# Two feature tiles per VectorE and ScalarE operation in the up stage of a hybrid block, with PSUM tiles of two banks there

## The chip, the cores and the metric

The kernel runs on one core of a Trainium2 chip. The metric is device time in microseconds (us) of one execution of the whole kernel. Five engines work side by side on that core, each with its own queue of instructions, taken in order: TensorE (PE in the profile) multiplies matrices, VectorE (DVE) and ScalarE (ACT) do arithmetic on whole tiles, GpSimd (POOL) and SyncE (SP) mostly issue DMA transfers between HBM (device memory) and the core's SBUF. Engines wait for one another through semaphores. TensorE writes its products into PSUM, which this kernel divides into eight banks, each a tile of 128 partitions by 512 float32 numbers.

## The reference

One layer of a transformer block on a sequence of 256 positions with 2048 features. Cut to the part that the change and the prediction touch:

```python
x = x + merged @ w_out[l]                          # o stage; merged: three gated attention branches

h2 = rms_norm(x, g_ffn[l])
u = causal_depthwise_conv(h2 @ w_up[l], conv_w[l], conv_b[l])   # up stage: 2048 -> 2 x 5632, 3 taps
u_gate, u_val = jnp.split(u, 2, axis=-1)
x = x + (jax.nn.silu(u_gate) * u_val) @ w_down[l]  # down stage: 5632 -> 2048
```

`causal_depthwise_conv` makes each feature at position s from the same feature at positions s, s-1 and s-2 with three factors of that feature and a bias. Inputs and outputs are float32.

## The kernel before, in words

**Precision.** A float32 product is made of products of split numbers: `hi` is the number cast to the shorter type fp32r, `lo` the remainder. `piece()` (L137) brings 128x1024 weights in by one DMA of SP's queue (`raw`), lets ScalarE cast them into `hi` (L143) and VectorE subtract to get `lo` (L144). There are four buffers of each. Where weights are already on the chip or come by another way, `parts()` does the same (L378, L379).

**Stages.** The kernel works through its matrix products one after the other: the projections (names in g, f, s, b, kv), attention, the gates, the o stage (names with `o`), the up stage (names with `u`), and the down stage (names with `d`). The o and the down stage are made by `blocked()` (L423) for two column halves `nb` of 1024: some pairs of weight rows are multiplied plainly (`eight`, four accumulators X), others by a scheme with seven products in place of eight (`seven`, with four more accumulators Y). When the last product of seven is issued, `gather()` (L404) adds Y into the residual `xres`; at the end of a half L1213 adds X into `xres` on VectorE. All accumulators are PSUM banks.

**The up stage** (L1303 to L1327) goes through 11 groups of four feature tiles. For each group there are two sweeps, s=0 for the gate half of the features and s=1 for the value half. A sweep loads eight pieces of `w_up`; a piece serves two k steps (128 of the 2048 input features each) and four feature tiles. For each of these there are two matmuls: L1318 multiplies `hi` of the weights by [hi | lo] of `hT`, 512 columns (256 positions, both parts of the split), and L1319 multiplies `lo` of the weights by the hi part, 256 columns. They add up in one bank per feature tile, `u<f>_<s>`: left half and right half of a bank are two sums that have to be added. With two sweeps of four banks, all eight are in use by turns.

When a sweep is issued, one `conv` per feature tile is put into a list of side work with `later()` (L97); `tick()` (after each piece) takes the next step of it. `conv` reads the bank: ScalarE copies its right half (L1253), VectorE adds the left half (L1254), and multiplies by `rbc` (L1263), the row factor of the RMS norm, the same for all features. The result lies in `u_0` or `u_1`, tiles with two zeros ahead of position 0. Then come the taps with factors that belong to a feature: ScalarE's L1268 (third factor and bias), VectorE's L1269 and L1270. The gate half ends with SiLU (L1272). The value half is multiplied into it (L1276), and `split_to` (L175) splits the product into hi (L177) and lo (L178) for the down stage.

**What sets the order.** Most instructions stand in each queue in the order that the program issues them, fixed by `pin()` and `in_order()`. The first group is special, since `hT` and `rbc` are not ready: `hidden_T(n)` (L1176) makes a quarter of `hT`. It transposes `xres` on TensorE into banks (`transposed`, L191), and ScalarE and VectorE split it from there (L184, L186). Its last two quarters are made while the first sweep runs, as side work between pieces. After them POOL writes the row factors to DRAM and reads them back spread over all partitions: that is `rbc` (L1186, L1187).

**PSUM.** One pool `pp` of eight one-bank tiles, from the start to the end of the kernel (L81). A new tile takes the next bank in turn and waits for what was done with that one bank:

```python
    pp = ctx.enter_context(tc.tile_pool(name="pp", bufs=8, space=bass.MemoryType.PSUM))

    def bank(name):
        return pp.tile([P, 512], F32, tag="bank", name=name)
```

## Time and profile before

| | |
|---|---|
| median of three runs | 1457.79 us (1457.63 to 1458.24) |
| span of the profiled execution, the kernel's time in that execution | 1457.8 us |
| mean DMA rate | 270 GB/s |
| instructions on TensorE, VectorE, ScalarE | 7289, 1824, 1222 |
| stages by TensorE's instructions | o stage ends at 742.5, up stage 742.5 to 1232.5, down stage from there to 1453.8 |

The profiled execution's own time is its span, and that is the median to within 0.01 us. In the rows that follow, a line such as "L1318 PE MATMUL u<-hT,hi_u" names the line of the kernel, the engine, the operation, its output and its inputs (numbers of buffers left out). In a group's row the numbers behind "|" are the busy time of the group, the mean duration of one instruction in ns, the idle time of that engine just ahead of these instructions, and what ended most of that idle time. In a row of the timeline the first number is the start, the second the duration. A row of the stretches begins with the window and its length; then come busy time and count for TensorE's matmuls, its weight loads, VectorE, ScalarE and POOL, the granted clock of TensorE (1.00 is full speed), the busy share of the DMA engines, and GB/s.

### The profile page before, as it was taken

How to read it: one execution, taken by the hardware profiler on the slowest of the kernel's cores; microseconds unless marked ns; L12 is line 12 of the kernel's file. 1: busy time of each engine (PE TensorE's matmuls, PEld its weight loads, DVE VectorE, ACT ScalarE, POOL GpSimd, SP SyncE). 2: the span in 40 equal slices, each digit the busy share in tenths (PEclk: the TensorE clock that was granted, in tenths of full speed). 3: DMA queues.
4: the chain of work that ended last, by engine and by line, in shares of the span. 5: the costliest groups of instructions: out<-in, count | busy, mean ns of one | idle time of the engine just before them, and what ended most of it. 6: DMA issues, size and time to landing. Idle time of an engine off the chain costs nothing.

```text
span 1457.8 us, 20647 instructions
## 1 busy us (share of the span) xinstructions
PE 1451.5 (100%) x7289; PEld 1227.1 (84%) x7289; DVE 1229.2 (84%) x1824; ACT 857.5 (59%) x1222; POOL 33.0 (2%) x70
## 2 busy tenths in 40 slices
PE   9999999999999999999999999999999999999998
PEld 7888888888888888888888888888888888888887
DVE  5788778776898899998987988888888877999988
ACT  6755445464554555546776656556556556676775
POOL 0000011010000000000000000000000010000000
PEclk9999999999999999999999999999999999999999
DMA  8797899777668576788877888888888899789996
GB/s 296 227 350 245 324 324 328 266 247 221 206 201 272 181 219 207 264 271 254 302 226 221 294 274 300 282 276 295 284 280 291 275 260 255 253 288 341 326 334 236
DMA packets 169415, 393.41 MB, mean 270 GB/s; under 512 B 12907, under 2 KB 30207, under 8 KB 165087
## 3 DMA queue, kind: packets, MB, share of 16 engines
q1 hardware_dynamic: 165822, 384.87, 79.3%
q0 software_dynamic: 2160, 5.12, 1.8%
q10 hardware_dynamic: 1328, 2.11, 0.4%
q8 instruction: 57, 0.93, 0.2%
q14 instruction: 48, 0.39, 0.1%
HBM read 353.24 MB, written 43.00 MB: 272 GB/s over the span
## 4 chain that ended last, share of the span: by engine, by line
PE 95%; DVE 1%; issue 1%; DMA 1%; POOL 0%; ACT 0%; DVEq 0%; POOLq 0%; ACTq 0%
PE u L1318 22%; PE u L1319 11%; PE xd L386 3%; PE xd L384 3%; PE xd L385 3%; PE xg L386 3%; PE xg L384 3%; PE xg L385 3%; PE s L386 2%; PE s L384 2%; PE f L384 2%; PE f L385 2%; PE f L386 2%; PE b L386 2%; PE s L385 2%; PE b L384 2%
## 5 line engine op out<-in xcount | busy, mean ns | idle before, releaser
L1318 PE MATMUL u<-hT,hi_u 128*128 128x512 f32 x1232 | 428.4, 394 | 0.0
L1319 PE MATMUL u<-hT,lo_u 128*128 128x256 f32 x1232 | 341.3, 277 | 0.0
L144 DVE TENSOR_TENSOR lo_u<-raw_u,hi_u 128x1024 fp32r<-128x1024 f32 x176 | 215.4, 1225 | 72.4 <-ACT hi_u L143 72.3
L1318 PEld LDWEIGHTS u<-hT,hi_u 128*128 128x128 f32 x1232 | 231.0, 188 | 53.5
L143 ACT CAST hi_u<-raw_u 128x1024 fp32r<-128x1024 f32 x176 | 184.7, 1050 | 130.1 <-PE u L1318 95.5
L1319 PEld LDWEIGHTS u<-hT,lo_u 128*128 128x128 f32 x1232 | 231.3, 188 | 0.0
L379 DVE TENSOR_TENSOR lo_d<-raw_d,hi_d 128x1024 fp32r<-128x1024 f32 x88 | 106.9, 1223 | 13.2 <-ACT hi_d L378 11.1
L378 ACT CAST hi_d<-raw_d 128x1024 fp32r<-128x1024 f32 x88 | 91.8, 1054 | 36.7 <-PE xd L385 11.9
L378 ACT CAST hi_g<-raw_g 128x1024 fp32r<-128x1024 f32 (+1 forms) x80 | 77.1, 972 | 49.8 <-PE xg L385 17.0
L379 DVE TENSOR_TENSOR lo_g<-raw_g,hi_g 128x1024 fp32r<-128x1024 f32 (+1 forms) x80 | 88.8, 1122 | 4.1 <-ACT hi_g L378 4.1
L384 PE MATMUL xg<-hi_g,xT 128*128 128x512 f32 x175 | 68.1, 389 | 0.0
L386 PE MATMUL xg<-lo_g,xT 128*128 128x512 f32 x175 | 68.1, 389 | 0.0
L385 PE MATMUL xg<-hi_g,xT 128*128 128x512 f32 x175 | 68.1, 389 | 0.0
L143 ACT CAST hi_f<-raw_f 128x1024 fp32r<-128x1024 f32 (+1 forms) x40 | 38.6, 968 | 46.4 <-PE f L385 29.9
L1318 PE MATMUL u<-hT_rest,hi_u 128*128 128x512 f32 x176 | 62.0, 394 | 0.0
L1268 ACT ACTIVATE y<-u,taps 128x256 f32<-128x256 f32 x88 | 49.6, 596 | 19.0 <-DVE u L1263 18.9
L144 DVE TENSOR_TENSOR lo_s<-raw_s,hi_s 128x1024 fp32r<-128x1024 f32 (+1 forms) x40 | 44.7, 1124 | 18.5 <-ACT hi_s L143 18.5
L143 ACT CAST hi_b<-raw_b 128x1024 fp32r<-128x1024 f32 x32 | 33.7, 1053 | 45.0 <-PE b L385 21.1
L144 DVE TENSOR_TENSOR lo_f<-raw_f,hi_f 128x1024 fp32r<-128x1024 f32 (+1 forms) x40 | 44.4, 1118 | 17.1 <-ACT hi_f L143 16.9
L143 ACT CAST hi_s<-raw_s 128x1024 fp32r<-128x1024 f32 (+1 forms) x40 | 38.2, 960 | 34.3 <-PE s L385 18.8
L378 ACT CAST hi_t_d<-raw_t_d 128x1024 fp32r<-128x1024 f32 (+1 forms) x54 | 43.5, 835 | 18.7 <-PE xd L385 11.6
L378 ACT CAST hi_t_g<-t_g 128x1024 fp32r<-128x1024 f32 x30 | 31.5, 1051 | 38.9 <-PE xg L385 35.6
(555 smaller groups left out, 3552.4 us busy)
## 6 DMA issues: line engine op xcount, KB each, us to landing
raw_u<-in_w_up_dram SPq DMA_DIRECT2D x176, 512.0 KB, 5.0
raw_g<-in_w_in_dram SPq DMA_DIRECT2D x96, 512.0 KB, 4.6
raw_d<-in_w_down_dram SPq DMA_DIRECT2D x61, 512.0 KB, 5.5
pre_d<-in_w_down_dram SPq DMA_DIRECT2D x17, 1024.0 KB, 7.8
kept_d<-pre_d SPq DMA_DIRECT2D x17, 1024.0 KB, 6.5
raw_f<-in_w_in_dram SPq DMA_DIRECT2D x32, 512.0 KB, 5.7
raw_s<-in_w_in_dram SPq DMA_DIRECT2D x32, 512.0 KB, 5.8
raw_t_d<-kept_d SPq DMA_DIRECT2D x27, 512.0 KB, 5.8
```

Of the source, the lines that this page charges most:

```text
L143: pin(nc.scalar.copy(hi[:, :m], raw[:, :m]))
L144: pin(nc.vector.tensor_tensor(lo[:, :m], raw[:, :m], hi[:, :m].bitcast(F32), ALU.subtract))
L378: nc.scalar.copy(hi[:, :n], src)
L379: nc.vector.tensor_tensor(lo[:, :n], src, hi[:, :n].bitcast(F32), ALU.subtract)
L384: fix(nc.tensor.matmul(o, lhsT=ah, rhs=w[0], start=first, stop=False))
L385: fix(nc.tensor.matmul(o, lhsT=al, rhs=w[0], start=False, stop=False))
L386: fix(nc.tensor.matmul(o, lhsT=ah, rhs=w[1], start=False, stop=last))
L1268: nc.scalar.activation(y, u[:, 2:], AF.Identity, scale=tap(2), bias=tap(3))
L1318: nc.tensor.matmul(ps[i], lhsT=hi[:, j, c], rhs=hT(k + j), start=first, stop=False)
L1319: nc.tensor.matmul(ps[i][:, :S], lhsT=lo[:, j, c], rhs=hT(k + j)[:, :S], start=False, stop=last)
```

## The change

In the up stage, VectorE and ScalarE take two feature tiles in one operation wherever no factor of a single feature is in it: the copy of the right half, the addition of the left half, the multiplication by `rbc`, SiLU, the product of gate and value, and the split into hi and lo. The taps stay at one operation per feature tile. PSUM tiles in the up stage have two banks each, `[P, 2, 512]`, and the tiles `u_0`, `u_1` and `y` hold two features. The separate tile `cr` is gone: the copy writes to `u_0` or `u_1` at once.

The pool `pp` is closed ahead of the up stage and a pool `pu` with four two-bank tiles is opened (`new_banks`); `pu` is closed ahead of the down stage and `pd`, again with one-bank tiles, is opened. The four first tiles of `pu`, `first_0` to `first_3`, are taken at once. The first of the transposes of `hT` in the up stage go into `first_0` and `first_1`, and the first sweep into `first_3` and `first_2`. In the down stage Y takes the tag of one half of the pool and X that of the other, exchanged for the second column half.

```diff
@@ -78,10 +78,21 @@
     nc.gpsimd.memset(sm_pad, 0.0)
-    pp = ctx.enter_context(tc.tile_pool(name="pp", bufs=8, space=bass.MemoryType.PSUM))
-    def bank(name):
-        return pp.tile([P, 512], F32, tag="bank", name=name)
+    banks = [ctx.enter_context(ExitStack())]
+    pools = [banks[0].enter_context(tc.tile_pool(name="pp", bufs=8, space=bass.MemoryType.PSUM))]
+    def bank(name, tag="bank"):
+        return pools[0].tile([P, 512], F32, tag=tag, name=name)
+    placed = {}
+    def two_banks(i, name):
+        return placed.pop(i, None) or pools[0].tile([P, 2, 512], F32, tag=f"banks{i}", name=name)
+    def new_banks(name, n):
+        banks[0].close()
+        banks[0] = ctx.enter_context(ExitStack())
+        pools[0] = banks[0].enter_context(tc.tile_pool(name=name, bufs=n, space=bass.MemoryType.PSUM))
...
@@ -188,9 +199,9 @@
-    def transposed(dst, src, g, k, name, n=2):
-        ps = bank(f"{name}_{k}")
+    def transposed(dst, src, g, k, name, n=2, ps=None):
+        ps = bank(f"{name}_{k}") if ps is None else ps
         for j in range(n):
...
@@ -423,8 +434,10 @@
         wv = by_k(w)
-        X = [[bank(f"x{name}{nb}_{t}_{n}") for n in range(2)] for t in range(NT)]
-        Y = []
+        own = ("bank_a", "bank_b")[:: 1 - 2 * nb] if name == "d" else ("bank", "bank")
+        ys_of = lambda: [bank(f"y{name}{nb}_{j}", own[0]) for j in range(4)]
+        Y = ys_of() if name == "d" else []
+        X = [[bank(f"x{name}{nb}_{t}_{n}", own[1]) for n in range(2)] for t in range(NT)]
         ns = plan.count("s")
...
@@ -525,7 +538,7 @@
                         ready()
-                    Y += [bank(f"y{name}{nb}_{j}") for j in range(4)]
+                    Y += [] if Y else ys_of()
                 by_seven(sp[s], s == 0, s == ns - 1)
...
@@ -1175,8 +1188,12 @@
         yield 0 if n == 2 else 1
-        transposed(hT, xres, gffn, 4 * n, "hT")
-        transposed(hT, xres, gffn, 4 * n + 2, "hT")
+        at = [None, None]
+        if "up" in issued:
+            both = two_banks(n - 2, f"hT_{n}")
+            at = [both[:, i] for i in range(2)]
+        for i in range(2):
+            transposed(hT, xres, gffn, 4 * n + 2 * i, "hT", ps=at[i])
         square_part(ssf, xres, n, "f")
...
@@ -1243,63 +1260,66 @@
         for i in range(2):
-            u = cp.tile([P, S + 2], F32, bufs=1, name=f"u_{i}")
-            nc.vector.memset(u[:, 0:2], 0.0)
+            u = cp.tile([P, 2, S + 2], F32, bufs=1, name=f"u_{i}")
+            nc.vector.memset(u[:, :, 0:2], 0.0)
             pads.append(u)
...
     def out_of(ps, dst):
-        nc.scalar.copy(dst, ps[:, S:])
-        nc.vector.tensor_tensor(dst, dst, ps[:, :S], ALU.add)
+        nc.scalar.copy(dst, ps[:, :, S:])
+        nc.vector.tensor_tensor(dst, dst, ps[:, :, :S], ALU.add)
         return dst
     def y_tile(f, s):
-        return cp.tile([P, S], F32, tag="y", bufs=6, name=f"y_{f}_{s}")
+        return cp.tile([P, 2, S], F32, tag="y", bufs=3, name=f"y_{f}_{s}")
     def taken(cr, y, f, s):
-        ct = s * FT + f
-        u = pads[f % 2]
-        ins = nc.vector.tensor_tensor(u[:, 2:], cr, rbc, ALU.mult)
+        u = pads[f // 2 % 2]
+        ins = nc.vector.tensor_tensor(u[:, :, 2:], cr, rbc.unsqueeze(1).to_broadcast([P, 2, S]), ALU.mult)
         if y is not None:
         y = y_tile(f, s) if y is None else y
-        tap = lambda j: taps[:, j, ct : ct + 1]
-        nc.scalar.activation(y, u[:, 2:], AF.Identity, scale=tap(2), bias=tap(3))
-        nc.vector.scalar_tensor_tensor(y, u[:, 1 : S + 1], tap(1), y, ALU.mult, ALU.add)
-        nc.vector.scalar_tensor_tensor(y, u[:, 0:S], tap(0), y, ALU.mult, ALU.add)
+        tap = lambda j, i: taps[:, j, s * FT + f + i : s * FT + f + i + 1]
+        for i in range(2):
+            nc.scalar.activation(y[:, i], u[:, i, 2:], AF.Identity, scale=tap(2, i), bias=tap(3, i))
+        for i in range(2):
+            for j in (1, 0):
+                nc.vector.scalar_tensor_tensor(y[:, i], u[:, i, j : S + j], tap(j, i), y[:, i], ALU.mult, ALU.add)
         if s == 0:
...
             nc.vector.tensor_tensor(g, g, y, ALU.mult)
-            a_done.append(a_pair(f // 2)[:, f % 2])
+            a_done.append(a_pair(f // 2))
             split_to(a_done[-1], g)
-    def conv(ps, f, s):
-        taken(out_of(ps, cp.tile([P, S], F32, tag="cr", bufs=2, name=f"cr_{f}_{s}")), None, f, s)
-        return
-        yield
-    def first_convs(ps):
+    def convs(ps, f, s):
+        for i in range(2):
+            fi = f + 2 * i
+            taken(out_of(ps[i], pads[fi // 2 % 2][:, :, 2:]), None, fi, s)
+            yield
+    def first_convs(ps, f, s):
         kept = []
         padded()
-        for f in range(4):
-            kept.append(out_of(ps[f], y_tile(f, 0)))
-            if f % 2:
-                yield
+        for i in range(2):
+            kept.append(out_of(ps[i], y_tile(2 * i, 0)))
+            yield
         yield 3
-        for f in range(4):
-            taken(kept[f], kept[f], f, 0)
-            yield
-    def second_convs(ps):
+        for i in range(2):
+            taken(kept[i], kept[i], 2 * i, 0)
+            yield 1
+    def second_convs(ps, f, s):
         yield
-        for f in range(4):
-            deque(conv(ps[f], f, 1), 0)
-            yield 1
+        for _ in convs(ps, f, s):
+            yield 2
+    issued.add("up")
+    new_banks("pu", 1)
+    placed.update([(i, two_banks(i, f"first_{i}")) for i in range(4)])
     for f0 in range(0, FT, 4):
...
@@ -1307,7 +1327,8 @@
         for s in range(2):
-            ps = [bank(f"u{f0 + i}_{s}") for i in range(4)]
+            pairs_of = [two_banks((3, 2, 1, 0)[2 * s + i], f"u{f0 + 2 * i}_{s}") for i in range(2)]
+            ps = [pairs_of[i // 2][:, i % 2] for i in range(4)]
             c0 = s * D_FF + f0 * P
...
@@ -1320,15 +1341,12 @@
                 tick()
-            if f0 == 0:
-                later((first_convs, second_convs)[s](ps))
-                continue
-            for i in range(4):
-                later(conv(ps[i], f0 + i, s))
+            later((convs if f0 else (first_convs, second_convs)[s])(pairs_of, f0, s))
...
     dn = []
+    new_banks("pd", 4)
```

The names in the rows below: `xo1_t_n` are X of the second half of the o stage, `u0_0` to `u3_0` (before) and `first_3`, `first_2` (after) the accumulators of the first sweep of the up stage. A row ends with the engines whose semaphores the instruction waits for, a number at the end of a name is that of the buffer.

TensorE's queue where the o stage ends and the up stage begins, before:

```order
L386 MATMUL xo1_1_1_6346<-lo_o1_15_6718,mT_3_1_6043 128x512
L1318 MATMUL u0_0_6757<-hT_5957,hi_u0_0_0_6762 128x512 [waits Activation_49]
L1319 MATMUL u0_0_6757<-hT_5957,lo_u0_0_0_6763 128x256 [waits DVE_49]
L1318 MATMUL u1_0_6758<-hT_5957,hi_u0_0_0_6762 128x512
L1319 MATMUL u1_0_6758<-hT_5957,lo_u0_0_0_6763 128x256
L1318 MATMUL u2_0_6759<-hT_5957,hi_u0_0_0_6762 128x512 [waits DVE_49]
L1319 MATMUL u2_0_6759<-hT_5957,lo_u0_0_0_6763 128x256
L1318 MATMUL u3_0_6760<-hT_5957,hi_u0_0_0_6762 128x512 [waits DVE_49]
```

After, at the same place:

```order
L397 MATMUL xo1_1_1_6346<-lo_o1_15_6718,mT_3_1_6043 128x512
L1339 MATMUL first_3_6764<-hT_5957,hi_u0_0_0_6766 128x512 [waits DVE_49,PE_49,Activation_49]
L1340 MATMUL first_3_6764<-hT_5957,lo_u0_0_0_6767 128x256
L1339 MATMUL first_3_6764<-hT_5957,hi_u0_0_0_6766 128x512
L1340 MATMUL first_3_6764<-hT_5957,lo_u0_0_0_6767 128x256
L1339 MATMUL first_2_6763<-hT_5957,hi_u0_0_0_6766 128x512
```

The first product (L1318, now L1339) stands where it stood. Before, it had a wait for ScalarE's cast, and the products of the third and the fourth bank each had a wait for VectorE of their own. Now the first product has a wait for VectorE and one for TensorE's own earlier products besides, and those behind it have none.

VectorE's queue at that place, after (`xres_again` is the residual that L1230, before L1213, adds to; up to the second memset it is the order of before):

```order
L155 TENSOR_TENSOR lo_u0_0_4_6831<-raw_u0_0_4_6829,hi_u0_0_4_6830 128x1024 [waits DMAHW0_49,Activation_49]
L431 TENSOR_TENSOR e_1024_6733<-e_1024_6733,yo1_2_6465 128x512 [waits DVE_49]
L1230 TENSOR_TENSOR xres_again_5682<-xres_again_5682,xo1_1_0_6345 128x512 [waits PE_49]
L432 TENSOR_TENSOR xres_again_5682<-xres_again_5682,e_1024_6733 128x512 [waits DVE_49]
L155 TENSOR_TENSOR lo_u0_0_6_6874<-raw_u0_0_6_6872,hi_u0_0_6_6873 128x1024 [waits DMAHW1_49,PE_49,Activation_49]
L1230 TENSOR_TENSOR xres_again_5682<-xres_again_5682,xo1_1_1_6346 128x512 [waits DVE_49]
L1264 MEMSET u_0_7020 128x2x2
L1264 MEMSET u_1_7022 128x2x2
```

The last addition of the o stage, of `xo1_1_1`, stands behind five other operations here, two of them `lo_u`; it is the last use of a bank of the old pool on VectorE.

TensorE's queue where the up stage ends and the down stage begins (`xd0_t_n` are X of its first half), before:

```order
L1318 MATMUL u43_1_11540<-hT_rest_6863,hi_u40_1_14_11732 128x512
L1319 MATMUL u43_1_11540<-hT_rest_6863,lo_u40_1_14_11733 128x256
L384 MATMUL xd0_0_0_11754<-hi_d0_22_11760,aT_6753 128x512 [waits DMAHW5_49,DMAHW4_49,DMAHW6_49,DMAHW3_49,DMAHW7_49,DMAHW2_49,Activation_49]
L385 MATMUL xd0_0_0_11754<-hi_d0_22_11760,aT_6753 128x512
L386 MATMUL xd0_0_0_11754<-lo_d0_22_11761,aT_6753 128x512 [waits DVE_49]
```

After:

```order
L1339 MATMUL u42_1_11182<-hT_rest_6863,hi_u40_1_14_11360 128x512
L1340 MATMUL u42_1_11182<-hT_rest_6863,lo_u40_1_14_11361 128x256
L395 MATMUL xd0_0_0_11390<-hi_d0_22_11396,aT_6753 128x512 [waits DMAHW4_49,DMAHW5_49,DMAHW3_49,DMAHW6_49,DMAHW2_49,DMAHW7_49,DVE_49,Activation_49]
L396 MATMUL xd0_0_0_11390<-hi_d0_22_11396,aT_6753 128x512
L397 MATMUL xd0_0_0_11390<-lo_d0_22_11397,aT_6753 128x512
```

The first `xd` product had waits for ScalarE's cast and for DMAs, and has one for VectorE besides.

VectorE's queue at that place, from `lo_d0_24` on, after (`u40_1` and `u42_1` are the two tiles of the last value sweep):

```order
L390 TENSOR_TENSOR lo_d0_24_11473<-raw_d0_24_11470,hi_d0_24_11472 128x1024 [waits DMAHW4_49,PE_49,Activation_49]
L1271 TENSOR_TENSOR u_0_7020<-u_0_7020,u40_1_11181 128x2x256 [waits Activation_49]
L1279 TENSOR_TENSOR u_0_7020<-u_0_7020,rbc_5958 128x2x256 [waits DVE_49]
L390 TENSOR_TENSOR lo_d0_25_11491<-raw_d0_25_11488,hi_d0_25_11490 128x1024 [waits DMAHW5_49,PE_49,Activation_49]
L1288 SCALAR_TENSOR_TENSOR y_40_1_11415<-u_0_7020,taps_110,y_40_1_11415 128x256 [waits Activation_49] x2
L1288 SCALAR_TENSOR_TENSOR y_40_1_11415<-u_0_7020,taps_110,y_40_1_11415 128x256 [waits DVE_49] x2
L1271 TENSOR_TENSOR u_1_7022<-u_1_7022,u42_1_11182 128x2x256
L1294 TENSOR_TENSOR y_40_0_11208<-y_40_0_11208,y_40_1_11415 128x512 [waits DVE_49]
```

Here the additions that read the two last tiles of `pu` are the L1271 rows. The second of them, of `u42_1`, stands behind the first, the multiplication by `rbc`, `lo_d0_25` and four tap operations. Before, the four additions of the last four banks (L1254) stood in the same region, each behind its own copy.

## The prediction

> **What bounds the kernel now.** I read the busy totals first, then the chain of waits, the stretches, and the groups with what ended their idle time. All times are microseconds from the span's start.

> ```profile
> PE 1451.5 (100%) x7289; PEld 1227.1 (84%) x7289; DVE 1229.2 (84%) x1824; ACT 857.5 (59%) x1222; POOL 33.0 (2%) x70
> PE 95%; DVE 1%; issue 1%; DMA 1%; POOL 0%; ACT 0%; DVEq 0%; POOLq 0%; ACTq 0%
> ```

> TensorE is busy over the whole span, and 95% of the chain that ended last is TensorE's own instructions. A busy matmul row alone proves little, so the up stage needs a look of its own.

> ```profile
> 770.00:1000.00 230.00, 230.00 (x1329) 201.16 (x1328) 196.18 (x322) 138.57 (x213) 0.55 (x1) 1.00 0.84 282
> 1260.00:1450.00 190.00, 190.00 (x840) 157.29 (x839) 178.60 (x245) 131.23 (x170) 0.00 (x0) 1.00 0.90 309
> ```

> From 770 to 1000, inside the up stage, TensorE has no hole at all, at granted clock 1.00. VectorE is at 196 of 230 and ScalarE at 139 of 230. The down stage (1260 to 1450) has no hole either.

> ```profile
> L1318 PE MATMUL u<-hT,hi_u 128*128 128x512 f32 x1232 | 428.4, 394 | 0.0
> L1318 PEld LDWEIGHTS u<-hT,hi_u 128*128 128x128 f32 x1232 | 231.0, 188 | 53.5
> L143 ACT CAST hi_u<-raw_u 128x1024 fp32r<-128x1024 f32 x176 | 184.7, 1050 | 130.1 <-PE u L1318 95.5
> ```

> The up products (L1318) waited 0.0. The waiting goes the other way: ScalarE's cast of the next weight piece waited 95.5 for TensorE to free a buffer. VectorE and ScalarE run ahead by the four hi/lo buffers, so here they are not the bound.

> **The change, part by part.** *Fewer, wider operations.* Rows of today's operations, and of 128x512 ones of the same kind:

> ```profile
> L1254 DVE TENSOR_TENSOR cr<-cr,u 128x256 f32<-128x256 f32 x84 | 32.8, 419 | 0.0
> L1253 ACT COPY cr<-u 128x256 f32<-128x256 f32 x84 | 28.1, 366 | 13.8 <-PE u L1319 13.8
> L1272 ACT ACTIVATE y<-y 128x256 f32<-128x256 f32 x44 | 17.2, 415 | 6.6 <-DVE y L1270 6.3
> L255 DVE TENSOR_TENSOR pre_d<-pre_d 128x512 f32<-128x512 f32 x17 | 11.7, 690 | 0.3
> L410 ACT COPY e<-yo 128x512 f32<-128x512 f32 x2 | 1.2, 582 | 0.0
> L646 ACT ACTIVATE junk_f<-xres_again 128x512 f32<-128x512 f32 x8 | 5.0, 649 | 0.0
> ```

> VectorE has four tensor operations of this size per feature tile: two (L1254, L1263) for all 88 tiles and two (L1276, L178) for 44, 264 in all. At 0.42 each that is 110.9. After it are 132 at 0.69, 91.1: it saves about 20. ScalarE's 88 copies, 44 SiLUs and 44 casts become 44, 22 and 22; at 0.37 to 0.58 and 0.415 to 0.649 that saves about 15 (casts at the copy's price). The scaled operations (L1268 to L1270) stay 88 each. A read that crosses two PSUM banks stands in no row; it lies between one old operation (0.42) and two (0.84), and I take the 0.69 of the one-bank row. None of it is on the path, since TensorE waits 0.0 for these engines: **worth 0**. Even at 0.84, VectorE stays at its present 196 of 230, and the cover holds.

> *First new wait: the start of the up stage.* Before, each of the four banks of the first group is waited for alone. Now the first product waits for the last addition out of the old pool (L1213, `xo1_1_1`), as its order row's extra VectorE wait says; the value is the one that this addition sets. When is it done?

> ```profile
> 742.28 0.39 PE L386 MATMUL xo<-lo_o,mT 128*128 128x512 f32 x1
> 742.51 0.39 PE L1318 MATMUL u<-hT,hi_u 128*128 128x512 f32 x1
> ...
> 741.37 0.69 DVE L1213 TENSOR_TENSOR xres_again<-xres_again,xo 128x512 f32<-128x512 f32 x1
> ...
> 746.69 1.23 DVE L144 TENSOR_TENSOR lo_u<-raw_u,hi_u 128x1024 fp32r<-128x1024 f32 x1
> 747.83 0.69 DVE L1213 TENSOR_TENSOR xres_again<-xres_again,xo 128x512 f32<-128x512 f32 x1
> ```

> VectorE works without a pause from 741.37, and its order up to there is unchanged; all that it reads comes from products before 742.5. So the addition ends at 747.83 + 0.69 = 748.52, where TensorE went straight on at 742.51. It now stands for **6.0**. Queued behind it are all products; VectorE itself has 0.2 left to do. Bounds: 5.3, were the sum released at its start, and 6.7 with one operation more.

> *The transposes of hT* now come in three places instead of two, because the second half of a two-bank tile waits for VectorE's reading of the first. From the same durations, VectorE is done at about 757.3 (and 762.0 for the next), and TensorE arrives at about 757.3 (and 762.0). I take 0, and 0.5 as the upper end.

> *Second new wait: the start of the down stage.* The first `xd` product waits for L1271 (L1254 before) on the last pair, `u42_1`. Rows of before:

> ```profile
> 1231.65 0.28 PE L1319 MATMUL u<-hT_rest,lo_u 128*128 128x256 f32 x1
> 1232.34 0.28 PE L1319 MATMUL u<-hT_rest,lo_u 128*128 128x256 f32 x1
> 1232.46 0.39 PE L384 MATMUL xd<-hi_d,aT 128*128 128x512 f32 x1
> ...
> 1231.62 0.72 ACT L1253 COPY cr<-u 128x256 f32<-128x256 f32 x2 [0.40 <-PE u L1319]
> 1232.54 1.05 ACT L378 CAST hi_d<-raw_d 128x1024 fp32r<-128x1024 f32 x1 [0.20 <-PE u L1318]
> ...
> 1230.02 2.46 DVE L379 TENSOR_TENSOR lo_d<-raw_d,hi_d 128x1024 fp32r<-128x1024 f32 x2 [3.44 <-ACT hi_d L378]
> 1234.86 0.88 DVE L1269 SCALAR_TENSOR_TENSOR y<-u,taps,y 128x256 f32<-128x256 f32 x2
> ```

> In VectorE's new order L1271 of the last pair stands behind L1271 and L1279 of the pair before, one `lo_d`, and four scaled operations. The first pair's copy now waits for both its features; the product that starts at 1231.65 is the second's last, and today's copy began 0.3 after such a start, so the copy runs 1231.95 to 1232.55. The cast follows to 1233.6. VectorE: addition and multiplication 1232.55 to 1233.85 (0.6 to 0.7 each), `lo_d` (1.2) to 1235.0, four scaled operations (0.4 each, by the 0.88 for two) to 1236.65, the addition to 1237.3. TensorE would have gone on at 1232.46: it stands for **4.8**. Bounds: 4.5 if operations overlap as closely as these rows do, and 6.4 if a `raw_d` piece is late, as one was (1.6 beyond that).

> *The clock.* A hole of 5 to 6 is new for TensorE. The trace has one at its end:

> ```profile
> 1453.51 0.28 PE L386 MATMUL apart<-lo_d,a_ends 128*128 128x256 f32 x1
> 1452.00:1456.90 4.90, 1.79 (x14) 1.54 (x12) 1.80 (x3) 0.00 (x0) 0.00 (x0) 1.00 0.43 161
> 1457.10:1457.80 0.70, 0.00 (x0) 0.00 (x0) 0.00 (x0) 0.00 (x0) 0.00 (x0) 0.50 0.00 0
> 5.15 1.74 PE L781 MATMUL kv<-hi_kv,memT 128*128 128x512 f32 x4
> 6.72 0.63 PE L781 MATMUL kv<-lo_kv,memT 128*128 128x512 f32 x2
> ```

> The last product ends at 1453.8, and by 1457.1 the granted clock is 0.50: a hole of 3.3 was enough there. How long the half clock lasts after a hole no row shows directly. The nearest is the start: products began at 1.23 (L93), those from 5.15 still came 0.39 apart, and from 6.72 on 0.24. About 5.3 slow, half of it lost: 2.6. The price for one hole lies between 0 (no drop) and 3.4 (6.8 at half clock); I take **2.6 once**, for the longer hole.

> [...]

> **Sum.** 0 + 6.0 + 0 + 4.8 + 2.6 = +13.4. The profiled execution's span is 1457.8, equal to the median of the runs (1457.79), so 1457.8 + 13.4 = **1471.2**.

> **The rivals.**
> *No clock loss*: both waits, full clock. [...] Time 1457.8 + 10.8 = 1468.6.
> *A drop in both holes, or a third wait*: 1457.8 + 16.0 = 1473.8. The third wait would be VectorE's first multiplication by `rbc`, with split pieces queued behind it:

> ```profile
> 760.52 0.74 POOL L1186 DMA_DIRECT2D rstd_row<-scales  x1 [423.33 <-DVE scales L636]
> 770.68 0.55 POOL L1187 DMA_DIRECT2D rbc<-rstd_row  x1 [9.43 <-DMA rstd_row<-scales]
> rbc<-rstd_row POOLq DMA_DIRECT2D x1, 128.0 KB, 8.0
> ```

> Today rbc lands at 778.7. The later transposes push its start back by some 10, TensorE's holes by 6, so VectorE would stand about 5 there. The buffers ahead leave 0.3 to 1.5 at the next pieces: 0 is likeliest, 2 more possible.
> *Only the first wait bites* (the second is covered because ScalarE's and VectorE's queues are further ahead than I think): +6.0 to +8.6, 1463.8 to 1466.4. Against it: every operation in that sum reads or follows the last products.
> *Not slower.* If VectorE paced the products in the up stage, its 20 saved would come off: 1457.8 + 10.8 - 20 = 1448.6, and any 11 of them would make it even. The place is L144 ahead of L1319; it decides as soon as products wait for `lo_u`. Against it: 0.0 idle in L1318's row. For it only that a matmul row counts as busy what is queued; the weight loads' row shows 53.5 idle, which is the slack that one 512-wide product leaves after a 0.19 load.
> [...]
> *The change does not do what it says*: wide operations as dear as two. TensorE sees none of it, so the time stays 1471.2.

> **How the numbers follow.** Both waits and one drop 0.50 (1471.2); no drop 0.20 (1468.6); two drops or late rbc 0.16 (1473.8, up to 1476); one wait 0.07 (1465); within 0.2% of before 0.04, if the new waits are met before TensorE asks; faster 0.03. 0.2% (2.9) is about what a measurement here tells from no change. The range takes the first three with the bounds of the clock and of the second wait: 1465.0 to 1476.0. Slower 0.93, same 0.04, faster 0.03.

> **What would show it.** In the profile of the changed kernel: a hole of about 6 in TensorE ahead of the first `first_3` product, ended by VectorE's L1230; one of about 5 ahead of the first `xd`, ended by L1271; a granted clock of 0.50 for some 5 after the first; VectorE's busy time lower by about 20 and ScalarE's by 15, with TensorE's product spacing in between unchanged. I am wrong if the first product of either stage starts within 1 of the one before, if clock stays at 1.00, or if products in 800 to 1200 come closer together than before.

## The result and the profile after

| | before | changed |
|---|---|---|
| median (lowest to highest) | 1457.93 us (1457.63 to 1458.24, 4 runs) | 1474.18 us (1473.98 to 1475.40, 4 runs) |
| ratio, 95% interval | | 1.0111 (1.0099 to 1.0123) |
| span of the profiled execution | 1457.8 | 1472.2 |

The change makes the kernel 16.25 us slower. The page of the changed kernel, in its first section and its groups:

```profile
PE 1456.0 (99%) x7289; PEld 1230.6 (84%) x7289; DVE 1225.2 (83%) x1692; ACT 848.4 (58%) x1134; POOL 32.6 (2%) x70
...
L1339 PE MATMUL u<-hT,hi_u 128*128 128x512 f32 x1176 | 408.7, 394 | 0.0
...
L154 ACT CAST hi_u<-raw_u 128x1024 fp32r<-128x1024 f32 x176 | 184.8, 1051 | 148.2 <-PE u L1339 97.5
...
L395 PE MATMUL xd<-hi_d,aT 128*128 128x512 f32 x136 | 54.1, 398 | 4.8 <-issue 4.8
```

The up products still wait 0.0, and ScalarE's cast still waits for TensorE: in the middle of the stage nothing changed. New is a wait of 4.8 ahead of `xd` (L395), whose releaser the page could not name. The start of the up stage, on the timeline (start, duration):

```profile
740.78 0.39 PE L397 MATMUL xo<-lo_o,mT 128*128 128x512 f32 x1
747.16 0.76 PE L1339 MATMUL first<-hT,hi_u 128*128 128x512 f32 x1 [5.99 <-DVE u L1264]
747.72 0.41 PE L1340 MATMUL first<-hT,lo_u 128*128 128x256 f32 x1
747.93 0.63 PE L1339 MATMUL first<-hT,hi_u 128*128 128x512 f32 x1
...
746.33 0.68 DVE L1230 TENSOR_TENSOR xres_again<-xres_again,xo 128x512 f32<-128x512 f32 x1
746.96 0.07 DVE L1264 MEMSET u<- 128x4 f32 x2
```

The hole runs from 740.78 + 0.23 (the distance of two such products) to 747.16: 6.15. The first product follows the end of the last addition, 747.01. The row names L1264, a memset that happened to end at that moment; the wait itself is for L1230, which stands ahead of it. Behind the hole the first pair of products takes 0.77 and the next ones 0.64 (from 747.93 to 748.57) instead of 0.35. The start of the down stage:

```profile
1239.20 0.27 PE L1340 MATMUL u<-hT_rest,lo_u 128*128 128x256 f32 x1
1244.27 0.77 PE L395 MATMUL xd<-hi_d,aT 128*128 128x512 f32 x1 [4.80 <-issue]
...
1239.44 0.69 DVE L1271 TENSOR_TENSOR u<-u,u 128x512 f32<-128x512 f32 x1 [0.51 <-ACT u L1270]
1240.16 0.69 DVE L1279 TENSOR_TENSOR u<-u,rbc 128x512 f32<-128x512 f32 x1
1240.77 1.22 DVE L390 TENSOR_TENSOR lo_d<-raw_d,hi_d 128x1024 fp32r<-128x1024 f32 x1
1241.90 1.67 DVE L1288 SCALAR_TENSOR_TENSOR y<-u,taps,y 128x256 f32<-128x256 f32 x4
1243.49 0.68 DVE L1271 TENSOR_TENSOR u<-u,u 128x512 f32<-128x512 f32 x1
```

The hole is 1244.27 - 1239.32 = 4.95, and it ends 0.10 after VectorE's second L1271 (1244.17). Stretches behind the two holes (TensorE's busy time is the first column, the granted clock the third number from the right):

```profile
747.16:751.30 4.14, 4.14 (x13) 3.56 (x14) 0.00 (x0) 0.00 (x0) 0.00 (x0) 0.50 0.45 127
751.40:755.00 3.60, 3.60 (x23) 3.14 (x23) 1.23 (x1) 1.21 (x2) 0.00 (x0) 1.00 0.00 0
...
1242.90:1249.60 6.70, 5.33 (x13) 4.20 (x14) 5.90 (x12) 2.53 (x5) 0.00 (x0) 0.50 0.44 171
1249.75:1252.00 2.25, 2.25 (x11) 1.84 (x11) 2.22 (x4) 0.69 (x1) 0.00 (x0) 1.00 0.37 103
```

The clock is at 0.50 behind both holes, until 751.34 and 1249.68. Products ran at half clock for 4.2 and 5.4. With half of that lost this is an estimated 2.1 and 2.7, an upper estimate, since a pair of products slowed by a little under two (0.64 against 0.35); e4 below measures 2.0 and 2.5.

By the two traces the 14.4 between the spans is: -1.5 (the o stage ended earlier here, 740.78 against 742.28, where nothing differs), +6.15, +2.2 in the up stage (489.95 to 492.16), +4.95, +2.6 from the first `xd` product to the end. The -1.5 is chance: in the traces of all these kernels, which do the same up to there, the o stage's last product starts anywhere from 739.77 to 743.87. Without it 15.9 stand against the 16.25 between the medians; the 0.3 left is within the spread of the runs.

### The profile page after: what moved, and what is told of

Its sections match the earlier page's. It is cut to its first block, busy times and chain, and to the rows that moved or that the text cites. A ratio compares the mean times of both kernels' runs of the same rounds, so it can differ in the third digit from the quotient of the medians.

```text
span 1472.2 us, 20431 instructions
## 1 busy us (share of the span) xinstructions
PE 1456.0 (99%) x7289; PEld 1230.6 (84%) x7289; DVE 1225.2 (83%) x1692; ACT 848.4 (58%) x1134; POOL 32.6 (2%) x70
## 5 line engine op out<-in xcount | busy, mean ns | idle before, releaser
L1339 PE MATMUL u<-hT,hi_u 128*128 128x512 f32 x1176 | 408.7, 394 | 0.0
L1340 PE MATMUL u<-hT,lo_u 128*128 128x256 f32 x1176 | 325.8, 277 | 0.0
L1339 PEld LDWEIGHTS u<-hT,hi_u 128*128 128x128 f32 x1176 | 220.5, 188 | 51.3
L1340 PEld LDWEIGHTS u<-hT,lo_u 128*128 128x128 f32 x1176 | 220.6, 188 | 0.0
L390 DVE TENSOR_TENSOR lo_d<-raw_d,hi_d 128x1024 fp32r<-128x1024 f32 x88 | 106.6, 1222 | 14.4 <-ACT hi_d L389 11.6
L1288 DVE SCALAR_TENSOR_TENSOR y<-u,taps,y 128x256 f32<-128x256 f32 x176 | 73.6, 480 | 0.7 <-ACT y L1285 0.7
L395 PE MATMUL xg<-hi_g,xT 128*128 128x512 f32 x175 | 68.1, 389 | 0.0
L1339 PE MATMUL u<-hT_rest,hi_u 128*128 128x512 f32 x168 | 59.3, 394 | 0.0
L395 PE MATMUL xd<-hi_d,aT 128*128 128x512 f32 x136 | 54.1, 398 | 4.8 <-issue 4.8
```

The lines of the kernel that those rows point to most:

```text
L390: nc.vector.tensor_tensor(lo[:, :n], src, hi[:, :n].bitcast(F32), ALU.subtract)
L395: fix(nc.tensor.matmul(o, lhsT=ah, rhs=w[0], start=first, stop=False))
L1288: nc.vector.scalar_tensor_tensor(y[:, i], u[:, i, j : S + j], tap(j, i), y[:, i], ALU.mult, ALU.add)
L1339: nc.tensor.matmul(ps[i], lhsT=hi[:, j, c], rhs=hT(k + j), start=first, stop=False)
L1340: nc.tensor.matmul(ps[i][:, :S], lhsT=lo[:, j, c], rhs=hT(k + j)[:, :S], start=False, stop=last)
```

## The experiments

Each was compared with runs of the kernel before on the same chip (medians 1458.1 for e1 to e4, 1458.6 for e5 to e7).

**e1, the shared wait at the up stage alone.** The kernel of before, with the `new_banks` of the change; only this call is added ahead of the up loop:

```diff
+    new_banks("pu", 8)        # close the pool, open one with the same eight one-bank tiles
     for f0 in range(0, FT, 4):
```

> The kernel of before with its narrow operations; alone the pool of PSUM banks is closed and opened again, with the same eight one-bank tiles, at the start of the up stage. Theory (the lost time is shared waits and the clock after them): the first product waits for the last addition of xo1_1_1, a hole of 6.1 as in the changed kernel, and 2.0 at half clock behind it: +8.1, about 1466. Rival (the loss lies in the two-feature operations, in the late transposes of hT or in a late rbc): none of them is in this kernel, so it stays at 1458, or, if only the shared wait but no clock loss is its own, 1464.

Measured: 1466.90 (1466.47 to 1478.78, 6 runs), ratio 1.0071 (1.0048 to 1.0094), 8.8 more than before. Stretches of its profile, the hole and what lies behind it:

```profile
744.10:750.60 6.50, 0.15 (x1) 0.00 (x0) 6.42 (x11) 1.01 (x1) 0.00 (x0) 0.79 0.52 170
750.65:754.70 4.05, 4.05 (x13) 3.47 (x14) 0.00 (x0) 0.00 (x0) 0.00 (x0) 0.50 0.43 129
```

A hole of 6.5 in which VectorE works without a pause, then 4.1 at half clock, of which about half is lost: 6.5 + 2.0. With not one wide operation in it, this kernel has the first loss in full. (The profiled execution was the one of 1478.78; the last section says what was different in it.)

**e2, the shared wait at the down stage alone.** As e1, but with `new_banks("pd", 8)` ahead of the down stage only.

> The kernel of before with its narrow operations; alone the pool is closed and opened again, with the same eight tiles, at the start of the down stage. Theory: the first xd product waits for the addition of the last bank (L1254 of u43_1), which ended at 1238.87 where TensorE went on at 1232.46: a hole of 6.4 and 2.6 at half clock, +9.0, about 1467. Rival (the hole in the changed kernel is due to its wide operations being late): about 1458 here.

Measured: 1467.27 (1465.81 to 1467.61, 5 runs), ratio 1.0058 (1.0046 to 1.0070), 9.2 more. On its timeline:

```profile
1231.05 0.28 PE L1325 MATMUL u<-hT_rest,lo_u 128*128 128x256 f32 x1
1237.57 0.77 PE L390 MATMUL xd<-hi_d,aT 128*128 128x512 f32 x1 [6.24 <-issue]
...
1237.05 0.41 DVE L1260 TENSOR_TENSOR cr<-cr,u 128x256 f32<-128x256 f32 x1
```

The product starts 0.11 after the addition of the last bank ends (1237.46); the hole is 6.4, and the clock stays at half until 1242.89, 5.3 behind the product's start, of which about half is lost. The hole is longer by 1.5 than that of the changed kernel, whose wide operations come to their last addition sooner.

**e3, the wide operations without the shared waits.** All of the change, but a pool for each bank, and in the up stage one for each two-bank tile. `AT_UP` and `AT_DOWN` list, in order, the bank that each tile had before, renumbered so that pairs lie side by side:

```diff
-    banks = [ctx.enter_context(ExitStack())]
-    pools = [banks[0].enter_context(tc.tile_pool(name="pp", bufs=8, space=bass.MemoryType.PSUM))]
+    def new_banks(name, n, order=""):
+        banks.close()
+        at[:] = [int(c) for c in order][::-1]
+        pools[:] = [
+            banks.enter_context(tc.tile_pool(name=f"{name}{i}", bufs=1, space=bass.MemoryType.PSUM)) for i in range(n)
+        ]
...
+        return pools[at.pop()].tile([P, 512], F32, tag="bank", name=name)
...
-    new_banks("pu", 1)
+    new_banks("pu", 4)
...
-    new_banks("pd", 4)
+    new_banks("pd", 8, AT_DOWN)
```

> The changed kernel with all its two-feature operations and two-bank tiles, but with one pool for each bank (before the up stage, and in the down stage) and one for each two-bank tile (in the up stage), so that a tile waits for its own banks alone; the banks are those of before up to renumbering. Theory: both holes and both clock drops go, and the 20 that VectorE saves is worth nothing: 1457.9, within 1.5. Rival A (the saved VectorE time counts once the holes are gone): 1440 to 1452. Rival B (two-feature operations or the transposes cost something of their own): 1460 to 1466.

Measured: 1458.57 (1457.97 to 1467.53, 12 runs), ratio 1.0010 (0.9997 to 1.0024). Its timeline at the two places:

```profile
741.02 0.39 PE L403 MATMUL xo<-lo_o,mT 128*128 128x512 f32 x1
741.25 0.39 PE L1345 MATMUL first<-hT,hi_u 128*128 128x512 f32 x1
...
1231.34 0.27 PE L1346 MATMUL u<-hT_rest,lo_u 128*128 128x256 f32 x1
1231.45 0.40 PE L401 MATMUL xd<-hi_d,aT 128*128 128x512 f32 x1
```

No hole, and no gain: the wide operations are worth nothing that can be measured here, neither way. Ten of the twelve runs lie between 1457.97 and 1458.95, and for them both rivals fall. The other two took 1467.5; they have no profile, and the last section comes back to them.

**e4, the holes filled.** The changed kernel with matmuls on zeros ahead of the two waiting products:

```diff
+    def filled(o, n):
+        for _ in range(n):
+            in_order(nc.tensor.matmul(o, lhsT=idle[:, :P], rhs=idle[:, :384], start=True, stop=True))
...
+    filled(bank("filler")[:, :384], 30)
     new_banks("pu", 1)
...
+    filled(two_banks(3, "filler_d")[:, 0, :384], 24)
     new_banks("pd", 4)
```

> The changed kernel with matmuls on zeros, whose results nobody reads, put on TensorE ahead of the two first products that wait: 30 of 384 columns at the up stage, 24 at the down stage, at an estimated 0.16 each 4.8 and 3.8 of the holes of 6.1 and 5.0. Theory (a hole costs its length and, beyond it, a stretch at half clock): the products start when they did, but at full clock; 2.0 and 2.6 less than the changed kernel, about 1469.6. Rival (the slow products behind the holes are slow for another reason, such as empty buffers of weights or the first reads of a new bank): still 1474, with products 0.43 apart behind both holes.

Measured: 1471.47 (1469.19 to 1479.19, 6 runs), ratio 1.0104 (1.0081 to 1.0127). Stretches: what is left of each hole, and the products behind it.

```profile
747.50:749.05 1.55, 0.18 (x2) 0.03 (x1) 1.43 (x4) 0.00 (x0) 0.00 (x0) 1.00 0.44 170
749.06:752.50 3.44, 3.44 (x20) 3.00 (x21) 0.00 (x0) 0.51 (x1) 0.00 (x0) 1.00 0.48 157
...
1243.15:1244.28 1.13, 0.15 (x1) 0.02 (x1) 1.13 (x3) 0.00 (x0) 0.00 (x0) 1.00 1.04 397
1244.29:1249.00 4.71, 4.71 (x21) 3.88 (x22) 4.59 (x9) 3.27 (x5) 0.00 (x0) 1.00 0.37 145
```

TensorE still waits, but the clock stays at 1.00, and the up and the down stage are shorter by 2.0 and 2.5 than in the changed kernel (1239.23 - 749.06 = 490.2 against 492.2; 225.5 against 228.0). The products behind the waits are again the first into the new banks, and they are not slow; so the slow products behind a hole are the clock. What is left of the up and the down stage is 0.2 longer each than before (490.2 against 490.0, 225.5 against 225.3). The median fell by 2.7 to 3.0 only, less than the 4.5 of the two stages. The profiled execution, which took the median, shows why: its last o product started at 742.40, 1.6 after that of the changed kernel, and from the stage before to the product that waits it is 6.4 and 5.1 instead of 6.15 and 4.95. Two of the six runs were about 8 longer than the median, which the last section takes up.

**e5, only the start of each hole filled.** As e4, but 7 matmuls at each place.

> The changed kernel with only 7 of the matmuls on zeros ahead of each of the two products that wait, put right behind the last product of the stage before: TensorE is busy 1.1 longer (7 at the 0.163 that they took in e4), then idle for about 5.0 and 3.8. In the profile of the changed kernel the clock fell at 744.51, 1242.86 and 1471.55, which are 146 and 67 times 3.413 apart, and stayed at half for 6.83. Theory (the clock is looked at in windows of 3.413 that run by themselves; a window that is idle as a whole halves it): with that phase the last windows that end in the holes begin before the holes do, at 741.1 and 1239.4, so neither hole holds a whole one: no half clock, 1469.6, as in e4. Rival (a fixed threshold: the clock falls 3.3 to 3.4 after TensorE's last work): both holes are longer than that, so both drops come 1.1 later, 1474. Where a run reaches the hole over 0.6 late by chance, the theory has a drop in it too.

Measured: 1474.16 (1473.15 to 1477.05, 4 runs), ratio 1.0115 (1.0098 to 1.0131). The time is the rival's, but the trace shows neither mechanism. The windows lay otherwise here: a drop's time, less as many whole windows of 3.413 as fit, leaves a remainder of 2.58, where the changed kernel's first profile has 0.41 (there the first two drops, 744.51 and 1242.86, lie 498.35 apart, 146 times 3.413). And the clock dropped at 746.69 and at 1241.62: the first 5.5 after TensorE's last work, the second 2.5 after it, so the delay is not fixed; and the windows of 3.413 that ended there were not idle. Stretches, a window each:

```profile
743.27:746.69 3.42, 0.47 (x3) 0.45 (x4) 2.83 (x6) 0.00 (x0) 0.00 (x0) 1.00 0.53 162
739.86:743.27 3.41, 1.45 (x9) 0.60 (x7) 3.41 (x6) 1.05 (x1) 0.00 (x0) 1.00 0.50 160
1238.21:1241.62 3.41, 1.10 (x7) 0.45 (x5) 2.00 (x3) 1.79 (x3) 0.00 (x0) 1.00 0.93 346
```

The windows with 0.47 and 1.10 of work ended in a drop, the one with 1.45 did not. As a share of the window, 1.10 and 1.45 are 32% and 42% (the expectation of e8 below calls them 28% and 37%). In this execution the second hole was longer, too, since a `raw_d` piece came late (ScalarE's cast of `hi_d` waited 1.75 for its DMA): from 1238.00 to 1244.53, 6.5 with the filler in it.

**e6, the changed kernel again**, unaltered, beside e5.

> The changed kernel once more, on the same chip as e5 and e7. Theory: 1474.2 as before (+6.1 and +5.0 for the holes, +2.1 and +2.7 at half clock, +0.2 for the transposes). A rival has no other number here: it is the comparison for e5.

Measured: 1474.45 (1472.85 to 1475.08, 4 runs), ratio 1.0109 (1.0094 to 1.0124). Three windows in a row at its first hole:

```profile
741.90:745.32 3.42, 0.00 (x0) 0.00 (x0) 3.42 (x6) 0.00 (x0) 0.00 (x0) 1.00 0.54 178
745.32:748.73 3.41, 1.81 (x5) 1.59 (x6) 1.47 (x4) 0.00 (x0) 0.00 (x0) 0.50 0.63 209
748.73:752.14 3.41, 3.41 (x12) 2.90 (x11) 0.00 (x0) 0.00 (x0) 0.00 (x0) 0.50 0.07 26
```

The window with 1.81 of work did not bring the clock back, the full one did; at the second hole a window with 2.62 (77%) did not either. With yet another remainder (1.21) both holes lost clock again.

**e7, one more VectorE operation per feature tile**, in the kernel of before:

```diff
         nc.vector.tensor_tensor(dst, dst, ps[:, :S], ALU.add)
+        nc.vector.tensor_tensor(dst, dst, dst, ALU.max)
```

> The kernel of before with one more VectorE operation per feature tile in the up stage (the maximum of the tile with itself, 128x256): 88 at 0.42 are 37 more for VectorE, where the change saves 20. Theory (VectorE runs ahead of TensorE in the up stage, with 82 of 490 idle): 1458, within 2. Rival (VectorE paces the products): up to 37 more, 1495; half of that if it paces half of the stage.

Measured: 1458.32 (1457.54 to 1459.08, 10 runs), ratio 1.0000 (0.9991 to 1.0010). The up stage as one stretch, before and in e7 (the third group of numbers is VectorE's busy time):

```profile
742.00:1232.00 490.00, 490.00 (x2833) 428.63 (x2832) 408.14 (x667) 292.18 (x451) 13.90 (x20) 1.00 0.85 272
742.00:1232.00 490.00, 490.00 (x2832) 428.60 (x2831) 433.15 (x753) 292.36 (x450) 13.62 (x20) 1.00 0.82 271
```

VectorE's busy time there rises from 408.14 to 433.15, 25 and not the 37 that were expected, and TensorE does not notice. So VectorE does not pace the stage now, and would not with 25 more.

**e8, the clock by itself.** A program of bursts and holes:

```python
for i in range(6):
    for n in range(2, 10):
        busy(80 + 3 * i)                     # matmuls on zeros into one PSUM bank
        for _ in range(n):                   # the next burst waits for these reads
            nc.vector.tensor_tensor(c[:, :384], c[:, :384], burst[:, :384], ALU.add)
```

> A kernel of its own that measures the clock after holes; it leaves out the whole computation and writes zeros. TensorE runs 48 bursts of 80 to 95 matmuls on zeros (0.163 each, 13 to 15.5), and between two bursts it waits for a chain of 2 to 9 VectorE additions out of its PSUM bank, an estimated 0.6 each: holes from about 1.4 to 5.6, six of each length, at chance places in the windows of the clock. Theory, as the drops of the changed kernel, e1, e2, e5 and e6 suggest it (windows of 3.413 that run by themselves; a window busy for under about a third halves the clock, as the one with 28% in e5 did and the one with 37% there didn't; a window that is nearly all busy restores it, as 77% in e6 did not): all drops have one remainder against 3.413; holes under 2.2 never cause one, holes over 4.7 always, those between by their place. Rival A (the clock falls a fixed 3.3 to 3.4 after the last work): holes over 3.4 always cause a drop, shorter ones never, with no common remainder. Rival B (only windows idle as a whole count): holes of 3.5 to 5.6 cause one in 3 to 64 of 100 cases.

Measured: the clock dropped 32 times and came back 32 times, and all 64 moments have a remainder of 0.160 to 0.162 against 3.41333, the step that they give themselves: from the drop at 65.016 to the return at 918.348 are 853.33, 250 times 3.41333. The holes are counted, as above, from where the next product would have started. None of the 12 holes of 1.4 and 2.0 dropped the clock, 14 of the 18 of 2.6, 3.2 and 3.75 did, and all of the 18 of 4.3, 4.9 and 5.5. Windows on both sides of the two limits found (here the columns are TensorE, weight loads, VectorE, POOL):

```profile
508.75:512.16 3.41, 1.23 (x8) 0.78 (x8) 2.02 (x4) 0.00 (x0) 1.00 0.00 0
512.16:515.58 3.42, 3.42 (x13) 1.61 (x11) 0.00 (x0) 0.00 (x0) 0.50 0.00 0
525.81:529.23 3.42, 1.42 (x9) 0.74 (x8) 1.86 (x4) 0.00 (x0) 1.00 0.00 0
529.23:532.64 3.41, 1.83 (x12) 1.11 (x12) 1.46 (x3) 0.00 (x0) 1.00 0.01 2
211.79:215.20 3.41, 2.58 (x9) 1.24 (x9) 0.74 (x2) 0.00 (x0) 0.50 0.02 5
215.20:218.62 3.42, 3.42 (x12) 1.60 (x11) 0.00 (x0) 0.00 (x0) 0.50 0.00 0
867.15:870.56 3.41, 2.77 (x9) 1.28 (x9) 0.55 (x1) 0.00 (x0) 0.50 0.00 0
870.56:873.98 3.42, 3.42 (x22) 2.06 (x21) 0.00 (x0) 0.00 (x0) 1.00 0.00 0
```

Read them in pairs, a window and the one after it. With 1.23 of 3.41 busy the clock halved (the fullest window that did so, 413.17 to 416.58, has 1.32), with 1.42 it stayed; at half clock, 2.58 busy didn't bring it back, 2.77 did. Both rivals fall: drops came 2.3 to 5.2 after the last work, and behind windows with up to 1.32 of work in them.

## Why the prediction was right, and where it was not

**The path.** Forecast: TensorE bounds the kernel, VectorE and ScalarE run ahead, so the wide operations are worth 0. Shown by e3 (all wide operations, and a ratio of 0.9997 to 1.0024) and e7 (25 more for VectorE, and 0.9991 to 1.0010). The rival "not slower" falls with them.

**The savings' size.** VectorE was to save 20 and ScalarE 15; by the totals of the page it is 4.0 and 9.1, in e3 6 and 9. The step that was mis-sized multiplied durations of single operations. Operations of one engine overlap, as two rows of the timeline of before show:

```profile
1232.39 0.74 DVE L1254 TENSOR_TENSOR cr<-cr,u 128x256 f32<-128x256 f32 x2
1233.05 0.76 DVE L1263 TENSOR_TENSOR u<-cr,rbc 128x256 f32<-128x256 f32 x2
```

Two narrow operations take 0.66 from start to start of the next pair, 0.33 each, though one lasts 0.42; of the wide ones of 0.69, the next operation starts 0.61 later (1240.16 to 1240.77 above). 264 x 0.33 against 132 x 0.61 leaves 7. ScalarE's narrow copies overlap too: the 84 of L1253 in the prediction's row last 0.366 each, but are 28.1 busy, not 30.7. The durations of the wide operations themselves came as forecast, for the reads across two banks (L1271, L1270) too:

```profile
L1279 DVE TENSOR_TENSOR u<-u,rbc 128x512 f32<-128x512 f32 x42 | 28.9, 688 | 0.8
L1271 DVE TENSOR_TENSOR u<-u,u 128x512 f32<-128x512 f32 x42 | 28.7, 684 | 10.1 <-ACT u L1270 10.1
L1270 ACT COPY u<-u 128x512 f32<-128x512 f32 x42 | 24.5, 584 | 22.8 <-PE u L1340 22.8
```

**The first wait**, 6.0: measured 6.15, by the addition that was named. **The transposes**, 0: the up stage is longer by 2.2, of which 2.0 is clock by e4. **The second wait**, 4.8: measured 4.95, through the same chain; its upper bound, a late `raw_d`, came in e5. e1 and e2 show that each wait comes from reopening the pool, and not from the wide operations. The third wait, for `rbc`, did not come: between 752 and 1239 no product starts more than 0.15 later than its distance from the last one usually is.

**The clock** is the term that failed: "I take 2.6 once, for the longer hole". There were two drops, by e4 worth 2.0 + 2.5 = 4.5, and the rival with both (1473.8) was right at the lower chance. The shorter hole cost more than the longer one because of where they lie in the windows: the half clock lasted 6.83 both times, but the waiting product came 2.65 after the first drop (744.51) and 1.41 after the second (1242.86). The 1.9 that the sum lacks here are most of the 3.0 by which 1471.2 fell short; the rest is 0.3 in the two waits, 0.2 in the up stage and the spread of the runs. The 2.6 was the author's estimate, from slow products at the start of the kernel, where the trace of before has the clock at 1.00 (1.23 to 9.80), and no row of before shows its upper end, 3.4 (6.8 at half clock). What the changed kernel's trace shows in their place is 4.2 and 5.4 of products within 6.83 at half clock each, 2.0 lost behind the longer hole and 2.5 behind the other by e4. The prediction left open whether a hole of 5 or 6 halves the clock. In e8 that was no matter of luck: windows of 3.413 with up to 1.32 of work ended in a drop. By these two numbers, an estimate, a hole must put 2.1 of idle time into one window, and one of over 4.2 does that wherever it lies, since even split evenly between two windows it puts 2.1 into each; the holes of 4.3 and more in e8 did it 18 times in 18. Both holes here, 6.15 and 4.95, are longer. So one drop in two holes was not likely, and the forecast's time came close because the two waits, 11 of the 16, were right.

**The base.** The span was taken for the time of the execution. In every run since, the time lies 1.6 to 1.8 above the span (1473.98 against 1472.2 here, 1458.52 against 1456.8 in e3). So the profiled execution of before probably took 1459.5, 1.6 over the median; the 1.5 by which its o stage ended later would account for that. The forecast does not suffer, since its base is the median too. Added to the median, the terms measured by the traces give 1457.9 + 6.15 + 2.2 + 4.95 + 2.6 = 1473.8, where the runs show 1474.2.

## What to carry to other kernels

Here a PSUM pool that was closed and opened again turned separate waits per bank into one wait for everything that the old pool held; with the half clock behind it this cost 8.8 at the up stage alone (e1) and 9.2 at the down stage alone (e2). Where the next stage is to start at once, give each bank, or each group that is freed together, a pool of its own (e3). Before making an engine faster, look whether the bound engine ever waits for it. And price a hole in TensorE with its clock: in the traces of the changed kernel, e1, e2, e5 and e6, holes of 5 to 6.5 were followed by 3.4 to 6.0 of products at half clock, an estimated 1.6 to 2.8 beyond the hole's own length (by the pace of the products, 0.64 against 0.35), and in e4 and e8 no hole of up to 2.0 cost clock.

## What the runs showed of the hardware

**A second rhythm of the up products.** In the one execution of e1 with 1478.78, the products of the whole up stage came 1.9% slower. The same 400 us of both, first e1, then before:

```profile
800.00:1200.00 400.00, 400.00 (x2266) 346.81 (x2265) 339.82 (x556) 234.13 (x360) 3.89 (x6) 1.00 0.82 279
```

```profile
800.00:1200.00 400.00, 400.00 (x2309) 349.81 (x2309) 344.26 (x564) 236.58 (x363) 7.72 (x11) 1.00 0.86 283
```

The clock is 1.00 in both, and TensorE waits for nothing; 128 products take 22.61 instead of 22.19 from the start of the stage to its end, about 9 in all. Two of the 12 runs of e3 and two of the 6 of e4 are longer than their medians by 7.6 to 9.0, but were not profiled, so that they have this cause is a guess. What sets the rhythm stays open. All runs of the kernel before lie below 1460, so none of them is longer in this way, and whether the reopened pools bring it about is not tested. It has no part in the 16.25: in the two profiles of the changed kernel 128 products take 22.19, as before.
